# Row transposes on ScalarE's queue and half of the down products in 16 bits, in a decoder block with a mixture of experts

## The chip, the cores and the metric

The kernel runs on one core of a Trainium2 chip. The metric is the device time of one execution in microseconds (us). TensorE is PE in the profile (PEld is its weight load), VectorE DVE, ScalarE ACT, GpSimd POOL, SyncE SP.

## What is computed

One decoder block for 2048 tokens of width 1024, all float32. A first RMS norm, a projection, two token mixers (gated linear attention and causal pooling) merged by gates, and an output product added to x. Then a second RMS norm, whose rows feed a router (36 logits per token, one group of experts, the two best experts in it) and 32 experts of inner width 256:

```python
h2 = rmsnorm(x, norm2_g[l])
...
g_logits = (ht @ w_rg).astype(jnp.float32) + b_rg.astype(jnp.float32)
e_all = jnp.einsum('td,gde->tge', ht, w_re).astype(jnp.float32) + b_re.astype(jnp.float32)
...
return (jax.nn.silu(xb @ w_gate[e]) * (xb @ w_up[e])) @ w_down[e]
```

The expert rows are weighted, added to x by token, and normed once more.

## The kernel before

**Numbers in two halves.** A float32 operand is mostly kept as two float16 tiles, the rounded value (high half) and the rest (low half); a product is then three matmuls, high by high, high by low and low by high (`PASSES`). `msplit` (lines 1293 to 1298) does this to a tile of expert weights, 128 x 1024: ACT writes the high half (line 1296), DVE the low half (line 1297). Gate and up weights go that way (tiles `mst`, then `mwh`); the down weights (tiles `msd`) do not, and their products run in float32.

**Mixer, four blocks of 512 tokens.** `block` (line 887) runs for each. At its end `out_mm` computes the output product, 128 tokens (a tile, t0 to t3) at a time; `out_norm` stores the tile (`out_dram`), norms it (`normed`: sum of squares at line 240 on ACT, scaling at line 242 on DVE, high half at line 251 on ACT, low half at line 251 on DVE) and stores the halves (`h2d`) from POOL's queue. `out_turn` (line 869) calls `turn`, which transposes the two halves by DMA (line 259), two DMAs for each tile, on the queue named by `TQ`, that is SP's. SP's queue also carries all weight loads of the mixer (line 168), in the order in which they stand. `logits` (line 874) multiplies the transposed halves with the router's weights (line 881, tile `aux`). The logits of a block and its routing are done inside the next block, as fillers (`fill`) between the matmuls of its first projection (`seven_raw`, line 638). In the fourth block the order is another (`LAST`).

**Experts.** 32 experts in 16 pairs (`moe`, line 1220). The order within a pair is `PLAN`: S0 to S5 load and split the next pair's weights (`split1`), U and A are the gate and up products of one expert (`mo_up`, line 1391) and the activation (`mo_act`: sigmoid on ACT at line 1399, two products on DVE at lines 1400 and 1401), X are the transposes of the next pair's rows (lines 1335 and 1348), D0 and D1 the down product of 128 rows of either expert (`mo_out`, lines 1416 and 1419), D2 that of up to 56 more rows of each (`mo_rest`, lines 1428 and 1431: two products of 64 output rows side by side), F the last norm and the scatter. A scheduler in the compiler orders what is ready on each engine by its own estimates; the engines then keep that order. Pools hold 8 tiles `mst`, 8 tiles `mwh` and 8 tiles `msd`.

Of the kernel before, what the change touches and what calls it, by code (L numbers as in the profile page):

```python
# [8 lines left out]
F16 = mybir.dt.float16  # L9
BF16 = mybir.dt.bfloat16  # L10
I32 = mybir.dt.int32
AF = mybir.ActivationFunctionType
OP = mybir.AluOpType
# [3 lines left out]
D = 1024  # L17
# [5 lines left out]
CAP = 128 + RW  # L23
PW = 1024
EPS = 1e-6
WSC = 64.0
ASC = 16.0
DSC = 1.0 / (WSC * ASC)
RSC = 4096.0
# [7 lines left out]
class Mixer:  # L37
# [213 lines left out]
        self.done = [self.nc.scalar.activation(hh[0], x, AF.Copy).ins, eng.tensor_tensor(hh[1], x, hh[0], op=OP.subtract).ins]  # L251
        return hh

    def turn(self, hh, dst, dma):

        nc = self.nc
        if dma:
            for i in range(2):
                self.turning = getattr(nc, self.TQ).dma_start(dst(i), hh[i], transpose=True).ins
            return  # L260
        for i in range(2):
            pt = self.pp.tile([128, 1024], F16, name="acch", tag="acc", bufs=4)
            for k in range(KT):
                nc.tensor.transpose(pt[:, k * 128:(k + 1) * 128], hh[i][:, k * 128:(k + 1) * 128], self.identh)
            p3 = pt.rearrange("p (k t) -> p k t", k=KT)
            if i == 0:
                nc.scalar.activation(dst(i), p3, AF.Copy)
            else:
                nc.vector.tensor_copy(dst(i), p3)
# [598 lines left out]

    def out_turn(self, hh, dma):
        h2 = [self.bt([128, KT, 128], F16) for _ in range(2)]  # L870
        self.turn(hh, lambda i: h2[i], dma)
        return h2

    def logits(self, t, h2):
# [12 lines left out]
    def block(self, b, tail):  # L887
# [55 lines left out]
        if last:  # L943
# [15 lines left out]
            def fetch(i):  # L959
                with self.tc.issue_after(self.turning):  # L960
                    self.fetch(n, i)

            acts = {"m": lambda t: (mm(t, 0), mm(t, 1)) if t else mm(t, 1), "t": turn, "l": logits,
                    "n": lambda t: (mm(t, 0), mm(t, 1, lambda: turn(t - 1))),
                    "s": split, "f": fetch}
            for c in self.LAST.split():
# [11 lines left out]
        def wo1():  # L978
            wo[1] = [self.weight("wv", O0 + 4 + j) for j in range(4)]

        acts = {"m": lambda t: mm(t, 0), "n": lambda t: mm(t, 1), "t": turn, "w": lambda t: wo1(), "a": lambda t: self.p1a(), "b": lambda t: self.p1b(),
                "c": lambda t: self.p1c()}
        for c in self.OUT.split():
# [213 lines left out]
    def columns(self, T, nm, pool):  # L1197

        V = self.nc.vector
        p, n = T.shape[0], T.shape[2]  # L1200
        wsc = 1.0 / RSC if T.shape[1] > 2 else 1.0
        t = pool.tile([p, 2, n], F32, name="tj" + nm)
        ii = pool.tile([p, 2, n], I32, name="ti" + nm)
        w = pool.tile([p, n], F32, name="tw" + nm)
        l = pool.tile([p, 2, n], F32, name="tl" + nm)
        z = T[:, 0]
        V.scalar_tensor_tensor(t[:, 1], z, -1.0, z, op0=OP.mult, op1=OP.max)
        V.tensor_scalar(ii[:, 0], t[:, 1], 1.0, -1.0, op0=OP.max, op1=OP.add)
        V.tensor_scalar(t[:, 0], t[:, 1], 1.0, -1.0, op0=OP.max, op1=OP.add)
        V.tensor_scalar(t[:, 1], z, 0.0, OOB, op0=OP.is_equal, op1=OP.mult)  # L1210
        V.tensor_tensor(t[:, 1], t[:, 0], t[:, 1], op=OP.add)
        V.tensor_copy(ii[:, 1], t[:, 1])
        V.tensor_scalar(w, T[:, 1], wsc, None, op0=OP.mult)
        if T.shape[1] > 2:
            V.scalar_tensor_tensor(w, T[:, 2], wsc, w, op0=OP.mult, op1=OP.add)
        V.tensor_scalar(l[:, 0], z, 0.0, None, op0=OP.is_lt)
        return ii, w, l, t


    def moe(self):  # L1220
# [18 lines left out]
        with tc.manual_schedule(engines={getattr(E, e) for e in self.MANUAL}) if self.MANUAL else ExitStack():  # L1239
            for P in range(self.NP + 1):  # L1240
# [5 lines left out]
                for c in plan.split():  # L1246
                    f, d = {"U": (self.mo_up, 0), "V": (lambda s, h: self.mo_up(s, h, 0, 128), 0),
                            "W": (lambda s, h: self.mo_up(s, h, 128, CAP), 0), "A": (self.mo_act, 0), "D": (self.mo_down, 0), "F": (self.finish, 0),
                            "G": (self.finish, -1), "R": (self.rows, 2), "B": (self.base, 1), "X": (self.mo_x, 1),
# [19 lines left out]
    def weights(self, P):  # L1269

        return {"P": P, "e": [8 * (j % 4) + j // 4 for j in (2 * P, 2 * P + 1)], "W": {}, "F": {}, "X": {}, "H": {}, "ac": {}, "ps": {}}

# [9 lines left out]
    def split1(self, s, i):  # L1282
        if i in s["W"]:
            return
        if i not in s["F"]:
            self.fetch(s, i)
        s["W"][i] = s["F"][i] if i % 3 == 2 else [self.msplit(f, self.mw) for f in s["F"][i]]

    def split(self, s):
        for i in self.ORDER:  # L1290
# [1 line left out]

    def msplit(self, f, pool):
        nc = self.nc
        w = pool.tile([128, 2, PW], F16, name="mwh", bufs=8192 // PW)
        nc.scalar.activation(w[:, 0], f, AF.Copy, scale=WSC)  # L1296
        nc.vector.scalar_tensor_tensor(w[:, 1], f, WSC, w[:, 0], op0=OP.mult, op1=OP.subtract)  # L1297
        return w
# [4 lines left out]
        q = slice(c % PW, c % PW + n)  # L1303
        return w[c // PW][:, q] if a is None else w[c // PW][:, a, q]

    BST, BSD = 8192 // PW, 8192 // PW

    def rows(self, s, i):
        P = s["P"]
# [71 lines left out]
    def mo_up(self, s, h, lo=0, hi=CAP):  # L1381
        nc, mp = self.nc, self.mp
        W, xT = [s["W"][3 * h + i] for i in range(2)], s["xT"][:, h]
        pg, pu = s["pp"][h] if lo else (self.acc(), self.acc())
        s.setdefault("pp", {})[h] = pg, pu
        for o, ps in ((0, pg), (1, pu)):
            for c in range(2):
                for k in range(KT):
                    for i, (a, b) in enumerate(self.PASSES):
                        col = k * 256 + c * 128  # L1390
                        nc.tensor.matmul(ps[:, c * CAP + lo:c * CAP + hi], self.part(W[o], col, 128, a), xT[:, b, k, lo:hi],  # L1391
                                         start=k == 0 and i == 0, stop=k == KT - 1 and i == 2)
        s["ps"][h] = pg[:, :2 * CAP], pu[:, :2 * CAP]

    def mo_act(self, s, h):
        nc, mp = self.nc, self.mp
        pg, pu = s["ps"][h]
        sg = mp.tile([128, 2 * CAP], F32, name="sg", bufs=4)
        nc.scalar.activation(sg, pg, AF.Sigmoid, scale=DSC)
        nc.vector.scalar_tensor_tensor(sg, pg, DSC, sg, op0=OP.mult, op1=OP.mult)  # L1400
        nc.vector.scalar_tensor_tensor(sg, pu, DSC, sg, op0=OP.mult, op1=OP.mult)  # L1401
        s["ac"][h] = sg.rearrange("p (c t) -> p c t", c=2)

    def mo_down(self, s, i):
        x, o, w, l, nl = s["X"][i]
# [5 lines left out]
    def mo_out(self, s, i, x, w):  # L1411
        nc = self.nc
        for hf in range(2):
            ps = self.acc()
            for f in range(2):
                nc.tensor.matmul(ps, s["ac"][i][:, f, :128], self.part(s["W"][3 * i + 2], f * D + hf * 512, 512),  # L1416
                                 start=f == 0, stop=f == 1)
            xh = x[:, hf * 512:(hf + 1) * 512]
            nc.vector.scalar_tensor_tensor(xh, ps, w, xh, op0=OP.mult, op1=OP.add)  # L1419

    def mo_rest(self, s, x, w):

        nc = self.nc
        ps = self.acc()
        m = [(h, f) for h in range(2) for f in range(2)]
        for q, (h, f) in enumerate(m):
            for hf in range(2):
                nc.tensor.matmul(ps[hf * 64:(hf + 1) * 64], s["ac"][h][:, f, CAP - 64:],
                                 self.part(s["W"][3 * h + 2], f * D + hf * 512, 512),
                                 start=q == 0, stop=q == len(m) - 1, tile_position=(0, hf * 64))  # L1430
        nc.vector.scalar_tensor_tensor(x, ps, w, x, op0=OP.mult, op1=OP.add)

    def finish(self, s, i):
# [59 lines left out]
    def overflow(self):  # L1493

        nc, tc = self.nc, self.tc
        V = nc.vector
        mp = self.mp
        nt = self.NTT
        n = nc.values_load(self.tot[0:1, 0:1], min_val=0, max_val=2 * nt + NE,  # L1499
                           skip_runtime_bounds_check_because="counts of the rows bound it")  # L1500
        with tc.If(n > 0):
            with tc.For_i(0, n):
                T = lambda name, sh, dt=F32: mp.tile([128] + sh, dt, name="o" + name)
# [24 lines left out]
                for c in range(2 * nt):  # L1528
                    a = mp.tile([128, 128], F32, name="oA", bufs=1)
# [4 lines left out]
                ii, w, _, _ = self.columns(tb, "o", mp)  # L1534
                er = nc.values_load(ei[0:1, 0:1], engines=[mybir.EngineType.SP], min_val=0, max_val=NE - 1,
                                    skip_runtime_bounds_check_because="a count of at most 31")
                W = [[self.load(self.A["we"][bass.ds(er, 1), :, c:c + PW].rearrange("o p c -> p (o c)"), i == 2)
                      for c in range(i * 2048, (i + 1) * 2048, PW)] for i in range(3)]
                W = [[self.msplit(f, self.mw) for f in w] if i < 2 else w for i, w in enumerate(W)]
                x = self.mxs[0]  # L1540
                o = self.out, ii
                self.base1(x, o, True)
                h = self.mhs[0]
# [8 lines left out]
                s = {"W": W, "xT": xT, "ac": {}, "ps": {}}  # L1552
# [5 lines left out]
            n = nc.values_load(self.tot[0:1, 1:2], min_val=0, max_val=nt, skip_runtime_bounds_check_because="0 or all tiles")  # L1558
            with tc.For_i(0, n) as t:
                x = self.mxs[0]  # L1560
# [98 lines left out]
```

## Time and profile before

| | |
|---|---|
| time, median of 3 runs | 1652.97 us (1650.61 to 1653.81) |
| profiled execution | 1646.32 us, span 1644.5 us |
| PE busy | 1516.8 us (92% of the span) |
| PEld busy | 916.5 us (56%) |
| DVE busy | 1063.8 us (65%) |
| ACT busy | 648.3 us (39%) |
| POOL busy | 523.8 us (32%) |
| mean granted TensorE clock | 0.965 |

The four blocks of the mixer fill the first 1100 us or so, the router's tables and the start of the experts the next 90 us, the 16 pairs the stretch from about 1160 to 1628 us. "Busy" of PE is the union of its matmuls, which overlap, so that a full row does not by itself mean full speed; the granted clock stands beside it, 1.00 being 2.4 GHz and 0.50 1.2 GHz.

### The profile page before, as it was taken

The page shows a single profiled execution, that of the slowest core. Times are in us where ns is not written, and L with a number is a line of the kernel's source. Part 1 is how long each engine was busy: PE and PEld are TensorE (multiplying, and loading weights), DVE is VectorE, ACT ScalarE, POOL GpSimd, SP SyncE. Part 2 cuts the span into 40 slices and gives each one's busy share as a digit, 9 for nine tenths or more (in the row PEclk, how much of TensorE's full clock was granted, in tenths as well). Part 3 has the DMA queues.
Part 4 walks back from the last instruction along what each step waited for, and adds up shares of the span by engine and source line. Part 5 has one row for each costly group of instructions (what it writes and reads, how often), then busy time and mean ns, then how long its engine had stood idle before and what let it go on. Part 6 is the DMA issues. An engine that isn't in the chain of part 4 may idle for free. (4 is left out here: it accounts for less than half of the span.)

```text
span 1644.5 us, 27592 instructions
## 1 busy us (share of the span) xinstructions
PE 1516.8 (92%) x10635; PEld 916.5 (56%) x10635; DVE 1063.8 (65%) x1941; ACT 648.3 (39%) x1021; POOL 523.8 (32%) x499
## 2 busy tenths in 40 slices
PE   4889996998999999999998999996799999999995
PEld 2365442445844444854443764443678686877773
DVE  8999797356844446762624773337667777777772
ACT  5643454251122252122333121123456566666651
POOL 1044243312414311332412341031434434444431
PEclk9899999998999999999999999997899999999998
DMA  8866687999566969566879665668699999999940
GB/s 292 256 218 214 212 266 221 262 344 263 163 193 195 258 177 324 155 214 178 234 173 275 224 186 164 202 185 288 240 314 329 334 331 336 335 330 324 331 180 34
DMA packets 247336, 400.95 MB, mean 244 GB/s; under 512 B 154731, under 2 KB 159211, under 8 KB 247200
## 3 DMA queue, kind: packets, MB, share of 16 engines
q1 hardware_dynamic: 224672, 330.79, 65.0%
q0 software_dynamic: 22528, 68.35, 11.4%
q8 instruction: 85, 1.39, 0.3%
q14 instruction: 51, 0.42, 0.1%
HBM read 300.33 MB, written 75.50 MB: 229 GB/s over the span
## 5 line engine op out<-in xcount | busy, mean ns | idle before, releaser
L1391 PE MATMUL acc<-xT,mwh 128*128 128x184 f16 (+2 forms) x3264 | 248.9, 238 | 0.0
L1391 PEld LDWEIGHTS <-mwh 128*128 128x128 f16 x3264 | 243.7, 98 | 7.7 <-issue 7.5
L842 PE MATMUL acc<-w,bt 128*128 128x512 f16 x768 | 169.4, 382 | 9.2 <-ACT w L175 9.2
L859 PE MATMUL acc<-w,bt 128*128 128x512 f16 x768 | 168.8, 379 | 3.5 <-DMA bt<-bt 1.9
L1297 DVE SCALAR_TENSOR_TENSOR mwh<-mst,mwh 128x1024 f16<-128x1024 f32 x128 | 153.4, 1219 | 24.2 <-ACT mwh L1296 24.0
L1296 ACT ACTIVATE mwh<-mst 128x1024 f16<-128x1024 f32 x128 | 128.7, 1050 | 54.3 <-PE acc L1391 53.5
L522 PEld LDWEIGHTS <-w 128*128 128x128 f16 x1344 | 131.0, 99 | 33.7 <-issue 9.3
L842 PEld LDWEIGHTS <-bt 128*128 128x128 f16 x768 | 75.7, 99 | 102.3 <-issue 13.5
L339 PEld LDWEIGHTS <-hS 128*128 128x128 f16 x768 | 75.5, 98 | 95.3 <-issue 5.8
L859 PEld LDWEIGHTS <-bt 128*128 128x128 f16 x768 | 74.4, 98 | 95.6 <-issue 5.8
L176 DVE SCALAR_TENSOR_TENSOR w<-w 128x1024 f16<-128x1024 f32 x74 | 99.9, 1365 | 38.4 <-ACT w L175 38.4
L175 ACT ACTIVATE w<-w 128x1024 f16<-128x1024 f32 x74 | 75.3, 1030 | 116.1 <-DMA w<-in_wv_dram 39.3
L1416 PE MATMUL acc<-msd,sg 128*128 128x512 f32 x256 | 115.9, 605 | 0.3 <-DVE sg L1401 0.3
L847 POOL TENSOR_TENSOR et<-et 128x512 f32<-128x512 f32 x32 | 45.2, 1418 | 200.8 <-DVE et L845 167.0
L522 PE MATMUL acc<-hS,w 128*128 128x256 f16 x768 | 95.1, 277 | 4.5 <-DVE w L176 3.0
L339 PEld LDWEIGHTS <-hT 128*128 128x128 f16 x576 | 56.4, 98 | 71.3 <-issue 5.1
L769 ACT ACTIVATE bt<-et 128x512 f16<-128x512 f32 x48 | 30.0, 628 | 166.6 <-POOL et L847 104.2
L845 DVE SCALAR_TENSOR_TENSOR et<-acc,et 128x512 f32<-128x512 f32 x64 | 43.4, 689 | 76.5 <-PE acc L842 76.5
L339 PE MATMUL aux<-w,hS 128*128 128x512 f16 x384 | 89.7, 384 | 3.1 <-DVE et L757 2.5
L339 PE MATMUL acc<-w,hS 128*128 128x512 f16 x384 | 88.3, 379 | 0.0
L819 ACT ACTIVATE et<-et 128x512 f32<-128x512 f32 x64 | 39.6, 629 | 105.4 <-DVE et L348 105.3
L1416 PEld LDWEIGHTS acc<-msd,sg 128*128 128x128 f32 x256 | 47.8, 193 | 56.4 <-issue 46.8
(307 smaller groups left out, 2608.5 us busy)
## 6 DMA issues: line engine op xcount, KB each, us to landing
w<-wkeep SPq DMA_DIRECT2D x210, 512.0 KB, 4.5
mst<-in_we_dram SPq DMA_DIRECT2D x128, 512.0 KB, 6.2
wkeep<-w SPq DMA_DIRECT2D x70, 512.0 KB, 3.0
msd<-in_we_dram SPq DMA_DIRECT2D x64, 512.0 KB, 7.2
w<-in_wv_dram SPq DMA_DIRECT2D x40, 512.0 KB, 5.3
x<-in_x_dram SPq DMA_DIRECT2D x32, 512.0 KB, 5.9
out_dram<-x POOLq DMA_DIRECT2D x16, 512.0 KB, 8.2
h2d<-bt POOLq DMA_DIRECT2D x32, 256.0 KB, 6.2
```

The lines of the kernel that those rows point to most:

```text
L175: nc.scalar.activation(w[:, 0, c:], f[:, c:], AF.Copy, scale=WSC)
L176: nc.vector.scalar_tensor_tensor(w[:, 1, c:], f[:, c:], WSC, w[:, 0, c:], op0=OP.mult, op1=OP.subtract)
L339: nc.tensor.matmul(p, L[name](i, c, k), w[k // 2][:, a, (k % 2) * 512:(k % 2 + 1) * 512], start=k == 0 and m == 0, stop=k == 3 and m == 2)
L522: nc.tensor.matmul(ps[:, :h], w[:, i, k * 128:(k + 1) * 128], L[name](c, k), start=k == 0 and m == 0, stop=k == 3 and m == 2)
L842: nc.tensor.matmul(ps, lhs, w[k // 2][:, a, (k % 2) * 512:(k % 2 + 1) * 512], start=k == 0 and i == 0, stop=k == 3 and i == 2)
L845: nc.vector.scalar_tensor_tensor(x, ps, DSC * ASC, x, op0=OP.mult, op1=OP.mult)
L847: self.on('madd').tensor_tensor(x, x, s[t, 1], op=OP.add)
L859: nc.tensor.matmul(ps, self.mT[t][k // 4][:, 4 * c + k % 4], w[hf][k // 2][:, a, (k % 2) * 512:(k % 2 + 1) * 512], start=k == 0 and i == 0 ...
L1296: nc.scalar.activation(w[:, 0], f, AF.Copy, scale=WSC)
L1297: nc.vector.scalar_tensor_tensor(w[:, 1], f, WSC, w[:, 0], op0=OP.mult, op1=OP.subtract)
L1391: nc.tensor.matmul(ps[:, c * CAP + lo:c * CAP + hi], self.part(W[o], col, 128, a), xT[:, b, k, lo:hi], start=k == 0 and i == 0, stop=k == ...
L1416: nc.tensor.matmul(ps, s["ac"][i][:, f, :128], self.part(s["W"][3 * i + 2], f * D + hf * 512, 512), start=f == 0, stop=f == 1)
```

## The change

Two things are changed.

1. In the first three blocks `out_turn` gives the two transposes of each tile to ScalarE's queue; in the fourth they stay on SP's.
2. Of each pair, the first expert's down product (h = 0) runs on float16 halves, in three passes. Its down weights are split by `msplit` into a pool of 4 tiles, its activations are split into a tile `ac` (high half on ACT, low half on POOL). The second expert's stay float32. The pool of `msd` shrinks from 8 tiles to 6. The scale of the split weights (`WSC`) and activations (`ASC`) is taken back in the rows' weights (`DSC`) and, for the second expert, by leaving out a factor.

```diff
@@ turn, out_turn
-    def turn(self, hh, dst, dma):
+    def turn(self, hh, dst, dma, queue=None):
...
-                self.turning = getattr(nc, self.TQ).dma_start(dst(i), hh[i], transpose=True).ins
+                self.turning = getattr(nc, queue or self.TQ).dma_start(dst(i), hh[i], transpose=True).ins
...
-        self.turn(hh, lambda i: h2[i], dma)
+        self.turn(hh, lambda i: h2[i], dma, None if self.blk + 1 == self.NB else "scalar")
@@ columns
-        wsc = 1.0 / RSC if T.shape[1] > 2 else 1.0
+        wsc = DSC / RSC if T.shape[1] > 2 else DSC
@@ split1, msplit
-        s["W"][i] = s["F"][i] if i % 3 == 2 else [self.msplit(f, self.mw) for f in s["F"][i]]
+        s["W"][i] = s["F"][i] if i == 5 else [self.msplit(f, self.mq if i == 2 else self.mw) for f in s["F"][i]]
...
-        w = pool.tile([128, 2, PW], F16, name="mwh", bufs=8192 // PW)
+        w = pool.tile([128, 2, PW], F16, name="mwh", bufs=(8192 if pool is self.mw else 4096) // PW)
...
-    BST, BSD = 8192 // PW, 8192 // PW
+    BST, BSD = 8192 // PW, 6144 // PW
@@ mo_act
-        nc.vector.scalar_tensor_tensor(sg, pu, DSC, sg, op0=OP.mult, op1=OP.mult)
-        s["ac"][h] = sg.rearrange("p (c t) -> p c t", c=2)
+
+        nc.vector.scalar_tensor_tensor(sg, pu, 1.0 if h else DSC * ASC, sg, op0=OP.mult, op1=OP.mult)
+        sg = sg.rearrange("p (c t) -> p c t", c=2)
+        s["ac"][h] = sg
+        if h == 0:
+            ac = s["ac"][h] = mp.tile([128, 2, 2, CAP], F16, name="ac", bufs=2)
+            nc.scalar.activation(ac[:, 0], sg, AF.Copy)
+            nc.gpsimd.tensor_tensor(ac[:, 1], sg, ac[:, 0], op=OP.subtract)
+
+    def downs(self, s, h):
+
+        ac, w = s["ac"][h], s["W"][3 * h + 2]
+        for f in range(2):
+            for a, b in self.PASSES if h == 0 else ((None, None),):
+                yield ac[:, f] if h else ac[:, b, f], lambda hf: self.part(w, f * D + hf * 512, 512, a)
@@ mo_out, mo_rest
-            for f in range(2):
-                nc.tensor.matmul(ps, s["ac"][i][:, f, :128], self.part(s["W"][3 * i + 2], f * D + hf * 512, 512),
-                                 start=f == 0, stop=f == 1)
+            n = 5 if i == 0 else 1
+            for q, (a, w2) in enumerate(self.downs(s, i)):
+                nc.tensor.matmul(ps, a[:, :128], w2(hf), start=q == 0, stop=q == n)
...
-        m = [(h, f) for h in range(2) for f in range(2)]
-        for q, (h, f) in enumerate(m):
+        for q, (a, w2) in enumerate(x for h in range(2) for x in self.downs(s, h)):
             for hf in range(2):
-                nc.tensor.matmul(ps[hf * 64:(hf + 1) * 64], s["ac"][h][:, f, CAP - 64:],
-                                 self.part(s["W"][3 * h + 2], f * D + hf * 512, 512),
-                                 start=q == 0, stop=q == len(m) - 1, tile_position=(0, hf * 64))
+                nc.tensor.matmul(ps[hf * 64:(hf + 1) * 64], a[:, CAP - 64:], w2(hf),
+                                 start=q == 0, stop=q == 7, tile_position=(0, hf * 64))
```

(The overflow loop, which runs no iteration with these inputs' row counts unless an expert has too many rows, splits its down weights as well.)

What the change moves, at three places. First ACT, where the first block hands over to the second: line 240 is the sum of squares of t2 and then t3, line 251 the high half of t2 and then t3, line 259 the transposes of t0 (the first two), t1, t2 and t3.

```order
+L259 DMA_TRANSPOSE bt_2835<-bt_2761 128x8x128
+L259 DMA_TRANSPOSE bt_2836<-bt_2762 128x8x128
 L240 ACTIVATE bt_2866,nss_2867<-x_2600 128x1024
 L251 ACTIVATE bt_2873<-x_2600 128x1024
+L259 DMA_TRANSPOSE bt_2879<-bt_2829 128x8x128
+L259 DMA_TRANSPOSE bt_2880<-bt_2830 128x8x128
 L240 ACTIVATE bt_2910,nss_2911<-x_2655 128x1024
 L251 ACTIVATE bt_2917<-x_2655 128x1024
+L259 DMA_TRANSPOSE bt_2923<-bt_2873 128x8x128
+L259 DMA_TRANSPOSE bt_2924<-bt_2874 128x8x128
+L259 DMA_TRANSPOSE bt_2927<-bt_2917 128x8x128
+L259 DMA_TRANSPOSE bt_2928<-bt_2918 128x8x128
```

The eight transposes now stand between ACT's steps of the later tiles' norms. Second SP's queue at the same place; line 168 is a weight load, line 273 the load of a tile of x for the next block.

```order
 L168 DMA w_3426<-wkeep_79 128x2048
-L259 DMA_TRANSPOSE bt_2835<-bt_2761 128x8x128
-L259 DMA_TRANSPOSE bt_2836<-bt_2762 128x8x128
 L168 DMA w_3428<-wkeep_79 128x2x512
+L273 DMA x_4644<-in_x_dram 128x1024
 L168 DMA w_3534<-wkeep_79 128x2048
-L273 DMA x_4644<-in_x_dram 128x1024
-L259 DMA_TRANSPOSE bt_2879<-bt_2829 128x8x128
-L259 DMA_TRANSPOSE bt_2880<-bt_2830 128x8x128
 L273 DMA x_4787<-in_x_dram 128x1024
-L259 DMA_TRANSPOSE bt_2923<-bt_2873 128x8x128
-L259 DMA_TRANSPOSE bt_2924<-bt_2874 128x8x128
```

The transposes leave SP's queue (two more go behind the last row), and the loads behind them close up. Third DVE in the experts, from the end of one pair's D2 (line 1431) to the first gate tiles of a later pair. Before:

```order
L1431 SCALAR_TENSOR_TENSOR mx2_10495<-acc_13652,twr_10526,mx2_10495 128x512
L1460 TENSOR_TENSOR frs_13641<-frs_13641,tlm_10509 128x1
L1486 COPY frs_13663<-fss_13662 64x1
L1487 COPY frs_13663<-fss_13662 64x1
L1488 TENSOR_TENSOR fss_13662<-fss_13662,frs_13663 128x1
L1489 TENSOR_SCALAR frs_13663<-fss_13662 128x1
L1467 TENSOR_TENSOR y_13642<-mx1_10494,y_13642 128x1024
L1460 TENSOR_TENSOR frs_13663<-frs_13663,tlr_10527 128x1
L1297 SCALAR_TENSOR_TENSOR mwh_13682<-mst_13678,mwh_13682 128x1024
```

Now, at the same place of the changed kernel (its line 1443 is the old 1431, its 1298 the old 1297):

```order
L1443 SCALAR_TENSOR_TENSOR mx2_10495<-acc_13825,twr_10526,mx2_10495 128x512
L1298 SCALAR_TENSOR_TENSOR mwh_13883<-msd_13879,mwh_13883 128x1024
L1298 SCALAR_TENSOR_TENSOR mwh_13886<-msd_13881,mwh_13886 128x1024
L1479 TENSOR_TENSOR y_13815<-mx1_10494,y_13815 128x1024
L1498 COPY frs_13844<-fss_13843 64x1
L1499 COPY frs_13844<-fss_13843 64x1
L1298 SCALAR_TENSOR_TENSOR mwh_13863<-mst_13859,mwh_13863 128x1024
```

The two new splits of down weights stand between D2 and the pair's last norm, ahead of the next gate tiles.

## Rows read from the trace of the kernel before

**Rows 1.** Windows: start:end, us, busy (count) by engine, PEclk, DMA share, GB/s.

```profile
1250.00:1300.00 50.00, 50.00 (x504) 39.46 (x503) 37.58 (x63) 32.88 (x45) 19.28 (x21) 1.00 0.94 333
```

**Rows 2.** Timeline of PE, one pair: start us, us, engine, line, operation, tiles, count.

```profile
1313.73 15.12 PE L1391 MATMUL acc<-xT,mwh 128*128 128x184 f16 x189
...
1330.09 7.08 PE L1416 MATMUL acc<-msd,sg 128*128 128x512 f32 x16
...
1337.99 3.65 PE L1428 MATMUL acc<-msd,sg 128*64 128x512 f32 x16
...
1342.04 1.19 PE L1391 MATMUL acc<-xT,mwh 128*128 128x184 f16 x13
```

**Rows 3.** Waits of PE: waited for, us in total, times, longest us.

```profile
PE aux L881 <- DMA bt<-bt: 18.3, 7, 4.7
```

**Rows 4.** Timeline of PE, after the first, second and third block.

```profile
365.62 2.75 PE L638 MATMUL acc<-w,hS 128*128 128x512 f16 x12
...
380.62 0.21 PE L881 MATMUL aux<-wrh,bt 128*128 128x36 f16 x1 [4.72 <-DMA bt<-bt]
...
380.70 5.22 PE L638 MATMUL aux<-w,hS 128*128 128x512 f16 x12
...
634.36 4.44 PE L638 MATMUL aux<-w,hS 128*128 128x512 f16 x12
...
897.42 4.57 PE L638 MATMUL aux<-w,hS 128*128 128x512 f16 x12
```

**Rows 5.** Windows around those three bursts.

```profile
380.60:386.00 5.40, 5.38 (x24) 2.10 (x25) 0.04 (x1) 0.00 (x0) 0.00 (x0) 0.52 1.14 255
634.30:638.70 4.40, 4.40 (x22) 1.73 (x19) 0.20 (x1) 0.83 (x1) 0.00 (x0) 0.61 1.08 369
893.00:901.00 8.00, 4.47 (x33) 2.11 (x34) 2.62 (x6) 1.28 (x1) 0.00 (x0) 0.58 1.17 377
```

**Rows 6.** Timeline of SP's queue, after the first block.

```profile
359.30 10.01 SPq L259 DMA_TRANSPOSE bt<-bt  x2
...
371.48 7.86 SPq L259 DMA_TRANSPOSE bt<-bt  x2
...
380.07 6.11 SPq L259 DMA_TRANSPOSE bt<-bt  x4
```

**Rows 7.** Transposes on SP's queue by line: ns of issue min/median/max, first and last start.

```profile
L259 SPq DMA_TRANSPOSE bt<-bt x28: 1232/2188/8660, 359.3 to 1114.9; - x28
```
```profile
L771 SPq DMA_TRANSPOSE bt<-bt x48: 1232/1245/2527, 138.3 to 1088.4; - x48
```

**Rows 8.** DMA, 340 to 366 us: traffic; issues, KB each, median us to landing.

```profile
DMA packets 2958, 10.69 MB, mean 411 GB/s; under 512 B 353, under 2 KB 353, under 8 KB 2956
...
w<-wkeep SPq DMA_DIRECT2D x8, 512.0 KB, 15.7
out_dram<-x POOLq DMA_DIRECT2D x4, 512.0 KB, 10.2
...
bt<-bt SPq DMA_TRANSPOSE x1, 11.7
```

**Rows 9.** Timeline of ACT, after the first block: high halves of t0 and t1.

```profile
358.80 1.05 ACT L251 ACTIVATE bt<-x 128x1024 f16<-128x1024 f32 x1
...
364.31 1.06 ACT L251 ACTIVATE bt<-x 128x1024 f16<-128x1024 f32 x1 [3.42 <-DVE x L242]
```

**Rows 10.** Costliest groups: count, busy us, mean ns, idle us before, its releaser.

```profile
L842 PE MATMUL acc<-w,bt 128*128 128x512 f16 x768 | 169.4, 382 | 9.2 <-ACT w L175 9.2
L1297 DVE SCALAR_TENSOR_TENSOR mwh<-mst,mwh 128x1024 f16<-128x1024 f32 x128 | 153.4, 1219 | 24.2 <-ACT mwh L1296 24.0
L1296 ACT ACTIVATE mwh<-mst 128x1024 f16<-128x1024 f32 x128 | 128.7, 1050 | 54.3 <-PE acc L1391 53.5
L847 POOL TENSOR_TENSOR et<-et 128x512 f32<-128x512 f32 x32 | 45.2, 1418 | 200.8 <-DVE et L845 167.0
```

More of the change, by code (lines that the diff above doesn't have):

```diff
@@ L1538, in overflow @@
                       for c in range(i * 2048, (i + 1) * 2048, PW)] for i in range(3)]
-                W = [[self.msplit(f, self.mw) for f in w] if i < 2 else w for i, w in enumerate(W)]
+                W = [[self.msplit(f, self.mw if i < 2 else self.mq) for f in w] for i, w in enumerate(W)]
                 x = self.mxs[0]
```

## The prediction

> **What bounds the kernel now.** I began with the experts, because both halves of the change meet TensorE and most of its float32 work is there. The window of 50 us inside the pairs [rows 1] is to be read from left to right: PE is busy for 50.00 of 50.00 us at a granted clock of 1.00, that is at 2.4 GHz, while DVE has 37.58, ACT 32.88 and POOL 19.28. DMA is busy for 0.94 of it at 333 GB/s. So here a microsecond taken from PE is a microsecond of the kernel, as long as no other engine comes last. The timeline of one pair [rows 2] gives the period, 1342.04 - 1313.73 = 28.31 us, and what the down products have in it: D0 and D1 together 7.08 us, D2 3.65 us, all in float32. Per period DVE works 37.58 / 50 x 28.31 = 21.28 us, ACT 18.62, POOL 10.92.
>
> For the mixer I read the waits of PE. The largest wait on a DMA there is that of the router's logits for the transposed rows, 18.3 us in 7 waits [rows 3]. The timeline of PE at the three handovers between blocks [rows 4] shows a second price: a burst of twelve matmuls takes 2.75 us before the waits and 5.22, 4.44 and 4.57 us behind them, and the windows around these bursts grant a clock of 0.52, 0.61 and 0.58 [rows 5], so TensorE runs mostly at 1.2 GHz after having waited. That is 2.47 + 1.69 + 1.82 = 6.0 us more. Together 24.3 us hang on these transposes, and no more than that can be won from them.
>
> Why they are late is seen on SP's queue [rows 6]: the pair of t0 holds it for 10.01 us, that of t1 for 7.86, the last four for 6.11, 24 us in all. The same operation issued in quieter stretches (line 771) has a median of 1.245 us, and line 259's here 2.188 with 8.66 at most [rows 7]. Just before, the DMAs moved 411 GB/s, eight weight loads stood ahead on the same queue, landing 15.7 us after issue, and the first transpose took 11.7 us to land, while POOL's queue landed transfers of the loads' size in 10.2 [rows 8].
>
> **Part 2, the first expert's down product in 16 bits.** Half of D0 and D1 goes: 3.54 us. In its place stand 12 float16 matmuls of 128 x 512 (2 halves of the width, 2 chunks of the inner width, 3 passes). The same shape in the mixer costs 169.4 / 768 = 0.2206 us each [rows 10], so 2.65 us: -0.89. Half of D2 goes: 1.83 us. In its place stand 12 matmuls with 64 output rows. If two run side by side, as the float32 ones do in being 3.65 us where eight full ones would be 7.08, each costs 0.110: 1.32 us, -0.50. If they do not, they cost 2.65, +0.82. No row shows float16 matmuls of this shape; I take side by side, the nearest row being the same shape in float32, and keep the other end. The period falls by 1.39 to 26.92 us, and by 16 pairs 22.3 us. At the other end it is 0.07 x 16 = 1 us.
>
> What is added lies beside PE. Each pair has two more splits, 2 x 1.05 = 2.10 us on ACT and 2 x 1.22 = 2.44 on DVE, and the activations' own split: on ACT 1.05 x 368 / 1024 = 0.38 us, on POOL 1.42 x 368 / 512 = 1.02 [rows 10]. (368 columns are two times 184, the width of the gate and up products in [rows 2].) DVE comes to 23.72 of 26.92 us (88%), ACT to 21.10 (78%), POOL to 11.94 (44%). The same bytes in a shorter period need 333 x 28.31 / 26.92 = 350 GB/s, below the 411 that were reached [rows 8]. The activations' split is hidden by the second expert's gate and up products, half of the 15.12 us of both [rows 2], against 0.38 + 1.02 and the passing on. The splits of down weights stand on DVE between D2 and the next gate tiles; behind them wait the next pair's gate splits, by 2.44 us, and the last norm of the pair. I price this at nothing as long as DVE's 3.2 us of rest per pair absorbs it; that is the point of a rival below. The two `msd` tiles fewer cost nothing, because the tiles of the first expert are now free once they are split and no longer held until D2. The first pair has no period to save in, and the three-pass chains are longer; for these I take off 2.3 us: **-20**.
>
> **Part 1, the transposes on ACT.** 24 DMAs go from SP's queue to ACT's, and with them their issue time. Between which bounds: 1.25 us each as on the quiet stretches, or what they cost on SP here, up to 24 us per handover. The nearest row is that of line 259 itself, whose median is 2.19 us; ACT's queue carries no weight loads ahead of them, so I take 1.25 to 2.19.
>
> ACT has room, but not for nothing. t0's pair follows the high half of t1, which ends at 359.85 [rows 9], about when SP issues it today. Then ACT's square sum of t2 waits, by 2.5 to 4.4 us, and with it the chain to t2's high half (now 364.31 [rows 9]), behind which t1's pair stands. t1's pair is then issued between 368 and 374 and lands, with the 3 to 4 us that ACT's own steps and the transfer still want, at 374 to 377, where the logits get it now at 380.62 [rows 4]. **What is late next** is t2 and t3: their high halves move back by 5 to 9 us, so that their pairs are issued at about 376 to 383, where SP began at 380.07 [rows 6]. So t0's and t1's waits go nearly whole, and part of it comes back as a wait for t2. The loads behind them on SP close up; nothing on PE waits for these there. Bounds: 0, and -24.3. I take a bit over half: **-13**.
>
> **Sum.** -20 - 13 = -33 us. The profiled execution, 1646.3 us, becomes 1613.3; it lies 6.7 us below the median of the runs, 1653.0, on which the forecast is made: 1620.
>
> **Rivals.**
> - *The queue was not the cause.* If the transposes land late because all 16 DMA engines are full (411 GB/s [rows 8]) and not because of what stands ahead on SP's queue, part 1 is worth 0: 1633. For it speaks the 11.7 us landing with the DMAs full; against it the shorter landings of POOL's queue at the same time. The Trainium skill speaks for this rival ("DMA: Bandwidth & Descriptors", section "Issuing engines are not separate DMA queues"): DMAs of all issuing engines run on the same 16 DMA engines, and issuing from several saves only the sequencer's time. By that rule the 24 us of issue per handover could go and the landing could not; the trace agrees as to the full engines and, by POOL's 10.2 against 15.7, not as to the landing. Chance 0.16.
> - *Half of part 2 is lost* because DVE at 88% delivers the splits late now and then: -10 in place of -20: 1630. For it: DVE's split already waits 24.0 us for ACT's half [rows 10]. Chance 0.13.
> - *16-bit matmuls of 64 rows do not run side by side*: part 2 is -1: 1639. Chance 0.03.
> - *Slower: ACT is held by its own transposes.* If they cost on ACT what they cost on SP [rows 6], t0's pair ends at 370, and t2's square sum, t2's high half, t1's pair and so on follow in a chain: t3's pair would end at about 397, against 386 today. That is up to 8 us later in the logits per handover, +24 with -20: 1657. It decides from an issue time of some 3 us each. For it: ACT issues in order, and the chain of the norm runs through it. Against it: nothing stands ahead of them on that queue. Chance 0.05.
> - *Slower: DVE becomes the bound of the pair.* Its rest is now 28.31 - 21.28 = 7.03 us; if this rest is waiting in order that cannot be shortened, the period is 23.72 + 7.03 = 30.75, +2.44 x 16 = +39, with -13: 1679. It decides when over 5.4 of the 7.03 us must remain (26.92 - 23.72 = 3.2 are there for nothing, and 2.2 more use up both gains). Against it: PE's 50.00 of 50 shows that DVE waits for PE, not PE for DVE. Chance 0.04.
>
> **How the numbers follow.** The forecast has 0.59; its own range runs from all of part 1 and part 2 (1653 - 24.3 - 22.3 = 1606) to a third of part 1 (1629). The range 1606 to 1638 takes in the first two rivals and leaves out 0.12 of the others and a little of each end. About 0.2% (3.3 us) is what a measurement can tell from no change. Faster: 0.59 + 0.16 + 0.13 + 0.03, less 0.01 for bad mixtures: 0.90. Slower: 0.04 and most of 0.05: 0.07; the same, 0.03.
>
> **What the profile afterwards would show.** Right: DMA transposes of line 259 on ACT's queue at 1.25 to 2.2 us; the logits' wait for `bt` down from 18.3 to some 5 to 10 us; bursts of 2.75 us behind them for part of the handovers; a pair period of 26.9 us with PE still at 50 of 50; float16 down matmuls at 0.22 us and, in D2, at 0.11; DVE at some 88%. Wrong: issue times of 4 us and more on ACT, ACT steps of t2 and t3 later by 8 us or more; PE below 49 of 50 in a pair with waits on DVE or on the tile `ac`; a D2 of 4.5 us.

## The result and the profile after

The changed kernel takes 1676.53 us (median of 4 runs, 1672.07 to 1685.67) against 1653.12 before: ratio 1.0153, 95% interval 1.0128 to 1.0178. It is **slower by some 23 us**, where 1620 (1606 to 1638) was forecast. The profiled execution is longer than that of before by 32.3 us (spans 1676.8 and 1644.5), and the places below are for that pair of executions.

Where the time went is found by looking for the same matmul in both traces. The middle one of line 339's matmuls of the second, third and fourth block starts 10.2, 28.8 and 42.0 us later than before: each handover between blocks loses 10 to 19 us. The end of D2 of the first pair is 46.8 us later, of the last pair 32.0. So the mixer lost 42 us, the start of the experts 5, and the pairs won 15.

**The experts first.** The window in the pairs, as [rows 1], and the timeline of PE over one pair, as [rows 2]:

```profile
1350.00:1400.00 50.00, 50.00 (x546) 40.93 (x545) 44.32 (x70) 40.26 (x53) 26.44 (x24) 1.00 0.99 354
```
```profile
1325.84 1.88 PE L1441 MATMUL acc<-msd,sg 128*64 128x512 f32 x8
...
1345.05 2.76 PE L1431 MATMUL acc<-mwh,ac 128*128 128x512 f16 x12
1347.65 3.60 PE L1431 MATMUL acc<-msd,sg 128*128 128x512 f32 x8
...
1351.87 1.49 PE L1441 MATMUL acc<-mwh,ac 128*64 128x512 f16 x12
1353.19 1.88 PE L1441 MATMUL acc<-msd,sg 128*64 128x512 f32 x8
```

PE is still full, DVE at 89%, DMA at 354 GB/s. The twelve 16-bit matmuls take 2.76 us, those of 64 rows 1.49: they do run side by side. From D2 to D2 it is 1353.19 - 1325.84 = 27.35 us. But it does not stay there: six pairs on, the same piece of D2 starts at 1490.02 and then at 1518.53, 28.51 us apart, and PE falls below 50 of 50:

```profile
1450.00:1500.00 50.00, 49.05 (x485) 36.96 (x483) 42.53 (x67) 34.19 (x48) 27.05 (x24) 1.00 0.96 347
```

**The mixer.** The logits' wait, [rows 3], has not shrunk but doubled; the view by source line shows the transposes on ACT's queue, as [rows 7] on SP's:

```profile
PE aux L882 <- DMA bt<-bt: 38.4, 11, 8.8
```
```profile
L259 ACTq DMA_TRANSPOSE bt<-bt x24: 1248/1472/15171, 357.7 to 936.1; - x24
```

Half of them take under 1.5 us to issue, as hoped; the longest 15.17. What a long one does is seen in ACT's timeline after the first block, to be read beside [rows 9]:

```profile
357.67 1.36 ACTq L259 DMA_TRANSPOSE bt<-bt  x1
...
359.02 1.05 ACT L251 ACTIVATE bt<-x 128x1024 f16<-128x1024 f32 x1
360.77 7.85 ACTq L259 DMA_TRANSPOSE bt<-bt  x1
368.67 1.06 ACT L240 ACTIVATE bt<-x 128x1024 f16<-128x1024 f32 x1 [8.60 <-issue]
...
372.05 1.06 ACT L251 ACTIVATE bt<-x 128x1024 f16<-128x1024 f32 x1 [2.23 <-DVE x L242]
...
378.29 13.76 ACTq L259 DMA_TRANSPOSE bt<-bt  x4
```

The second transpose of t0 holds ACT for 7.85 us; the square sum of t2 waits 8.60 us for it, t2's high half comes at 372.05 (before: 364.31; the two steps in [rows 9] are the high halves of t1 and t2, not of t0 and t1), and the last four are issued until 392.05 (before: 386.18 [rows 6]).

The waits are not all of the loss. The windows from the last matmul of line 859 to the middle one of line 339 in the next block, at the second handover, before and after (columns as in [rows 1]):

```profile
608.57:763.43 154.86, 150.79 (x1011) 90.73 (x1009) 92.58 (x214) 32.12 (x82) 46.81 (x46) 0.99 0.71 218
```
```profile
618.77:792.22 173.45, 155.52 (x1011) 92.56 (x1009) 92.88 (x214) 32.22 (x82) 46.10 (x46) 0.94 0.70 194
```

As many matmuls (1011) keep PE busy for 4.7 us longer, at a granted clock of 0.94 in place of 0.99, and the other 13.9 us are idle. Over the three handovers PE is idle for 27 us more and busy for 15 us more.

Why is the transpose slow with nothing ahead of it? The DMA view of 362 to 366 us, while it is being issued, and of 390.5 to 392.5, by queue (packets, MB, share of 16 engines); q10 is ACT's, q1 SP's, q0 POOL's:

```profile
q1 hardware_dynamic: 352, 1.27, 77.4%
q0 software_dynamic: 80, 0.26, 16.1%
q10 hardware_dynamic: 354, 0.09, 10.0%
```
```profile
q10 hardware_dynamic: 2189, 0.54, 126.5%
```

Alone, ACT's queue moves 2189 packets in 2 us. Beside SP's loads it moves 354 in 4 us while SP moves 352: as many as SP, as if they went one by one in turn. Most of SP's are 4 KB (159 ns each), a transpose is 1024 packets of 256 bytes (18 ns). At 88 a microsecond one transpose would last some 12 us. **Theory A** is that queues with work take turns at the DMA engines, packet by packet. The Trainium skill has it as a rule ("DMA: Bandwidth & Descriptors", section "Queues, rings and completion order"): each DMA engine goes round between the queues that have work, a packet at a time. The counts, 354 to 352, agree. By theory A the loads behind a transpose on SP's own queue do not come between its packets, and POOL's stores still can.

And SP, which no longer issues these transposes, waits for them. Of its waits from 600 to 670 us these two did not stand there before:

```profile
SPq L273 <- DMA bt<-bt: 17.3, 1, 17.3
SPq L168 <- DMA bt<-bt: 12.4, 1, 12.4
```

Rivals: **B**, ACT's queue is itself slow at transposes; **C**, what counts is that ACT is held and the norms stand behind it, whoever shares the engines; **D**, what counts is that SP's loads and ACT's transposes now wait for each other.

### The profile page after: what moved, and what is told of

It reads as the page before. It is cut to its first block, busy times and chain, and to the rows that moved or that the text cites. A ratio compares the mean times of both kernels' runs of the same rounds, so it can differ in the third digit from the quotient of the medians.

```text
span 1676.8 us, 28015 instructions
## 1 busy us (share of the span) xinstructions
PE 1517.0 (90%) x10763; PEld 920.6 (55%) x10763; DVE 1102.2 (66%) x1973; ACT 682.5 (41%) x1069; POOL 564.0 (34%) x515
## 5 line engine op out<-in xcount | busy, mean ns | idle before, releaser
L1298 DVE SCALAR_TENSOR_TENSOR mwh<-mst,mwh 128x1024 f16<-128x1024 f32 x128 | 159.5, 1275 | 8.5 <-ACT mwh L1297 8.2
L842 PEld LDWEIGHTS <-bt 128*128 128x128 f16 x768 | 75.6, 98 | 100.4 <-issue 11.1
L522 PE MATMUL acc<-hS,w 128*128 128x256 f16 x768 | 100.4, 286 | 7.3 <-ACT w L175 2.3
L210 POOL TENSOR_TENSOR rms<-rms,mhalf 128x1 f32<-128x1 f32 (+1 forms) x44 | 39.7, 903 | 140.6 <-DVE rms L209 139.7
L770 POOL TENSOR_TENSOR bt<-et,bt 128x512 f16<-128x512 f32 x48 | 61.7, 1288 | 43.0 <-ACT bt L769 43.0
```

Of the source, the lines that this page charges most:

```text
L522: nc.tensor.matmul(ps[:, :h], w[:, i, k * 128:(k + 1) * 128], L[name](c, k), start=k == 0 and m == 0, stop=k == 3 and m == 2)
L770: self.on(lo).tensor_tensor(hl[:, 1], x, hl[:, 0], op=OP.subtract)
L842: nc.tensor.matmul(ps, lhs, w[k // 2][:, a, (k % 2) * 512:(k % 2 + 1) * 512], start=k == 0 and i == 0, stop=k == 3 and i == 2)
```

## Experiments

Ratios are to runs of the kernel before on the same chip, whose medians lay between 1647.6 and 1653.1 us.

**Each part alone.** `act_alone` is the kernel before with the edits of `turn` and `out_turn`; `down16_alone` the changed kernel with

```diff
-        self.turn(hh, lambda i: h2[i], dma, None if self.blk + 1 == self.NB else "scalar")
+        self.turn(hh, lambda i: h2[i], dma, None)
```

> The kernel before with the first part alone: the 24 transposes on ACT's queue. In the changed kernel the mixer ends 42 us later than before (10, 18.6 and 13.4 us at the three handovers) and the pairs win about 15. If the whole loss is made by the transposes (theory A: on a queue of their own their 1024 packets of 256 bytes each alternate with the 4 KB packets of SP's loads, and behind them stands ACT's norm chain), this kernel takes 1653 + 42 = 1695 us. Rival: part of the loss in the mixer comes from the second part (other tiles, other order); then under 1680.

> The changed kernel with the transposes back on SP's queue: the second part alone. From the changed profile: 16 pairs 15 us shorter, the start of the first pair 5 us longer: 1653 - 15 + 5 = 1643 us. If the mixer's delay was what made the first pair late, 1638. As forecast at first (-20): 1633. If the pairs lose their gain without part one: 1653.

Part one: 1694.7 us, ratio 1.0285 (1.0256 to 1.0314), some 46 us lost. Part two: 1636.51, ratio 0.9925 (0.9898 to 0.9952), 12.6 us won. So the whole loss is part one's. (The parts add up to +33, the change to +23; part one's runs spread from 1689 to 1711, and what is left was not followed.)

**Whose fault is the queue?** `loads_pool` leaves the transposes on SP and issues the loads of line 168 from POOL's queue:

```diff
-        nc.sync.dma_start(w[:, :, c:], self.C[self.kept[mat, i]][:, :, c:])
+        nc.gpsimd.dma_start(w[:, :, c:], self.C[self.kept[mat, i]][:, :, c:])
```

> The kernel before with the mixer's weight loads of line 168 issued from POOL's queue; the transposes stay on SP's. Theory A (two queues share the DMA engines packet by packet): now SP's transposes run beside loads of another queue and get slow as ACT's were, the longest issues 8 to 15 us, the pairs over 8 us wherever 4 KB packets flow, though nothing stands ahead of them on SP. Rival B (ACT's queue itself is slow at transposes): SP's take 1.25 to 2.2 us, since the loads that stood ahead are gone. The total is not forecast: POOL's norm steps stand behind its loads.

1729.13 us, in a single run whose total was not forecast; what counts is its trace. The view by source line, and the DMA view of 368 to 378 us, by queue:

```profile
L259 SPq DMA_TRANSPOSE bt<-bt x28: 1232/4802/12267, 361.8 to 1192.3; - x28
```
```profile
q0 software_dynamic: 1051, 3.70, 93.1%
q1 hardware_dynamic: 1052, 0.28, 12.5%
```

SP's transposes became slow (median 4.80 us, longest 12.27) although no weight load stood ahead of them: 1051 packets on POOL's queue, nearly all of loads, and 1052 on SP's, nearly all of transposes. B falls.

**Is holding ACT needed for the loss?** `late_two_act` gives ACT only t2's and t3's transposes, behind which no norm stands:

```diff
...
-        self.turn(hh, lambda i: h2[i], dma)
+        self.turn(hh, lambda i: h2[i], dma, "scalar" if t > 1 and self.blk + 1 < self.NB else None)
```

> The kernel before, with only the transposes of the last two tiles (t2, t3) of the first three blocks on ACT's queue: behind them stands no step of the norms. If the loss is mostly ACT held in front of its norm steps (theory C), at most 3 us per handover are left: 1650 to 1662. If it is the packets' sharing alone (theory A without C), the four take some 13 us where SP's took 6 to 10, 4 to 7 us per handover: 1665 to 1675. In both, issue times of 4 to 10 us where loads flow.

1675.32 us, ratio 1.0151 (1.0117 to 1.0185): at the upper end of theory A's range (just past it), 13 us outside C's. The logits' wait:

```profile
PE aux L881 <- DMA bt<-bt: 42.3, 11, 8.7
```

Two times from the timelines, in us after the block's last matmul of line 859, at the three handovers, tell holding and sharing apart:

| | end of t3's high half (ACT) | end of the last logits (PE) |
|---|---|---|
| before | 28.1, 18.8, 22.7 | 52.6, 39.2, 43.2 |
| the change | 36.6, 29.9, 27.4 | 60.5, 55.9, 53.8 |
| `late_two_act` | 28.1, 17.7, 22.7 | 55.4, 53.9, 53.3 |
| `act_gated` | 23.7, 18.4, 20.4 | (loads late) |
| `sp_stores` | 29.1, 14.8, 14.0 | 48.0, 36.8, 37.6 |

With the norms on time as before, 27.6 of the change's 35.2 us are still lost. So most of the loss does not need ACT to be held. What holding adds is not separated, because `late_two_act` also leaves half of the transposes on SP.

**Take the competitor away.** `act_gated` is part one alone; each load of line 168 that is written behind a tile's transposes waits until they have landed:

```diff
-        nc.sync.dma_start(w[:, :, c:], self.C[self.kept[mat, i]][:, :, c:])
+        ins = nc.sync.dma_start(w[:, :, c:], self.C[self.kept[mat, i]][:, :, c:]).ins
+        if self.gate is not None:
+            self.tc.add_manual_dep(ins, self.gate.name, mybir.DependencyInfo(
+                mybir.DependencyClass.Sync, mybir.DependencyReason.DATA), reason="gate")
...
+        self.gate = self.turning if self.blk + 1 < self.NB else None
```

> Part one alone, with every weight load of line 168 that is written behind a tile's transposes (of the first three blocks, up to the next block's second stage) made to wait until these have landed, as on SP's queue it would stand behind them. Theory A (three queues take turns packet by packet; without SP's loads only POOL's stores are left): the slow issues on ACT fall from 8 to 16 us to the 3 to 8 us of SP's queue and at least half of the 42 us goes: 1655 to 1673. Rival C (what counts is that ACT is held and that the norms stand behind it, whoever shares the engines): 1685 to 1700. If the loads are missed by PE more than the rows, more than 1700.

1746.3 us, ratio 1.0548 (1.0513 to 1.0582), the last case named. The view by source line, ACT's timeline after the first block (line 262 is the old 259, 243 the old 240), and PE's largest wait:

```profile
L262 ACTq DMA_TRANSPOSE bt<-bt x24: 1247/1680/8694, 353.2 to 969.4; - x24
```
```profile
354.71 1.27 ACTq L262 DMA_TRANSPOSE bt<-bt  x1
356.03 1.06 ACT L243 ACTIVATE bt<-x 128x1024 f16<-128x1024 f32 x1 [1.37 <-issue]
```
```profile
PE aux L641 <- DMA w<-wkeep: 125.3, 3, 45.2
```

On the point it was made for it is clear: t0's second transpose, 7.85, 15.17 and 12.22 us at the three handovers of the change, takes 1.27, 1.35 and 1.36; t2's square sum waits 1.37 us in place of 8.60; t3's high half is earlier than before (table). Without SP's weight loads ACT's queue is quick there. It is not quick throughout: the longest issue is 8.69 us, behind t3's high half, where POOL's stores and rows of x still flow. The total says nothing on that, because PE now waits 125 us for loads: too many were held back.

**Smaller packets.** `act_2kb` issues each load of line 168 as two (halves of 2 KB a packet), on top of part one; `sp_2kb` does the same to the kernel before.

```diff
-        nc.sync.dma_start(w[:, :, c:], self.C[self.kept[mat, i]][:, :, c:])
+        for k in range(2):
+            nc.sync.dma_start(w[:, k, c:], self.C[self.kept[mat, i]][:, k, c:])
```

> Part one alone again (24 transposes on ACT's queue), but each weight load of line 168 is issued as two, one for each half, so that its packets are 2 KB in place of 4 KB; the bytes are the same. Theory A (the transposes' packets alternate one by one with the other queue's packets): a transposed packet now waits for half as long, the slow issues fall from 8 to 16 us to some 5 to 8, and about half of the 42 us of loss goes: 1665 to 1680. If it is bytes that are shared, or ACT's queue that is slow, or only its being held: 1690 to 1700 as with 4 KB.

> The control for it: the kernel before, transposes on SP's queue, the same loads in two halves of 2 KB packets. The loads of SP's own queue still stand ahead and nothing alternates with them but POOL's stores: 1649, within 6 us either way. If 2 KB packets are slower for the loads, more, and that is then to be taken off the other run.

1695.92 (ratio 1.0298, 1.0272 to 1.0324) and 1654.09 (1.0036, 1.0016 to 1.0055). **A miss**: the longest issue is still 13.4 us and no time came back. The stores of POOL and the loads of x kept their 4 KB packets. In that issue (632.5 to 645.9 us) ACT's queue moves 910 packets and SP's 1000, again nearly one to one, and POOL's 441 take 38.9% of the engines' time; whether smaller stores would help was not tried. The size of the loads' packets alone is no lever here.

**Other ways to turn the rows.** `pe_turns` is `down16_alone` with the transposes of the first three blocks on PE; `sp_stores` is `down16_alone` with POOL's stores of these blocks on SP's queue, so that no other queue is left at the handovers:

```diff
-        self.nc.gpsimd.dma_start(self.out[rows, :], self.xo[t])
+        (self.nc.gpsimd if self.blk + 1 == self.NB else self.nc.sync).dma_start(self.out[rows, :], self.xo[t])
...
-                nc.gpsimd.dma_start(store[:, i, :], hh[i])
+                (nc.gpsimd if self.blk + 1 == self.NB else nc.sync).dma_start(store[:, i, :], hh[i])
```

> The second part of the change, and in the first three blocks the row transposes on PE (16 matmuls of 128 x 128 for each tile and copies by ACT and DVE) and not by DMA at all: 12 tiles x 16 x 0.06 = 11.5 us more on PE, 24 us of waits and half clock less: 1636 - 12 = 1624. Rival: the copies stand in ACT's and DVE's norm chain and PE waits for them in place of the DMA: 1636 or more.

> The second part alone, with the stores of the first three blocks (rows of x and their normed halves) on SP's queue in place of POOL's: at the handovers SP's is then the only queue, and no transposed packet alternates with another queue's. Theory A: transposes that have come to their turn take 1.25 us each, the largest issue is below 4 us but for the loads ahead; the total may fall below 1637 by up to 10 us, unless SP, held by stores that wait for the norm, brings the loads late: then 1640 to 1660.

`pe_turns`: 1665.76, ratio 1.0104 (1.0085 to 1.0124), the rival: PE now waits for ACT's high halves, 22.3 us in 7 waits, in place of the DMA. `sp_stores`: **1618.02 us, ratio 0.9799 (0.9782 to 0.9815), faster than both kernels.** Its transposes and the logits' wait:

```profile
L259 SPq DMA_TRANSPOSE bt<-bt x28: 1232/1707/4095, 361.4 to 1100.8; - x28
```
```profile
PE aux L882 <- DMA bt<-bt: 12.4, 8, 6.2
```

The longest issue is 4.10 us (8.66 in [rows 7]), the logits end 2.4 to 5.6 us earlier at each handover, as theory A would have it. But the run moves a second thing. DVE's scaling of a tile (line 242) waits for the tile's store to land; the kernel before, then `sp_stores`:

```profile
DVE x L242 <- DMA out_dram<-x: 25.8, 7, 7.0
```
```profile
DVE x L242 <- DMA out_dram<-x: 13.4, 5, 7.1
```

With the stores on SP's queue this wait falls to about half, and t3's high half is 4.0 and 8.7 us earlier at the second and third handover (table). What shorter issues and what earlier stores won was not separated. Two runs on it:

> The changed kernel (transposes on ACT's queue, 16 bits) with the stores of the first three blocks on SP's queue: against the run with the stores and the transposes on SP (1618) only the queue of the transposes differs. Theory A: SP's loads and stores still take turns with ACT's packets and ACT is still held in front of its norm steps: slow issues of 5 to 12 us remain, 1640 to 1662. Rival: POOL's stores alone made ACT's transposes slow: 1616 to 1625, no slow issues.

> The kernel before with nothing changed but the stores of the first three blocks, on SP's queue. If the gain of the run with stores and 16 bits (1618 against 1637 with 16 bits alone) is the transposes' and independent of the experts: 1651 - 18 = 1633. If half of it came from the experts (its late pairs kept 27.2 us for longer): 1637 to 1642.

`act_sp_stores`: 1683.06, ratio 1.0206 (1.0161 to 1.0251); its longest issue is 7.61 us and yet it is slower than either side forecast. The length of the issues is thus not all that counts: summed over the 24 transposes of the handovers they take 82.8 us on SP's queue before, 95.6 in the change and 73.8 here, less than before. What the trace shows beside them is waiting between the queues (D): the first transpose of t2 has been issued on ACT at 654.1, its low half is done on DVE at 654.5, and the second is issued only at 664.09; SP's loads wait 15.8 us for transposes to land in that handover. Such waits of SP stand at every handover of the change (9.1, 29.7 and 20.1 us) and at none before or in `sp_stores`. How much of the loss is theirs, and what imposes them, was not tried: D stays open beside theory A. `stores_alone`: 1640.54, ratio 0.9930 (0.9913 to 0.9947), 10.8 us of the 18 expected and inside the range for half of the gain being the experts' (1637 to 1642). From the first D2 to the last the pairs take 403.1 us in `sp_stores` and 406.9 in `down16_alone`, so some 4 us are theirs. The 16 bits on top of `stores_alone` are worth 1640.5 - 1618.0, some 22 us.

**Why the late pairs stretch.** In `pool_mult` the product of the last norm goes from DVE to POOL for two of three row tiles, in `act_cast` a copy of the row transposes from DVE to ACT, in `stores_ac_dve` (on `sp_stores`) the activations' low half from POOL to DVE:

```diff
-        nc.vector.tensor_tensor(y, x, y, op=OP.mult)
+        (nc.gpsimd if i < 2 else nc.vector).tensor_tensor(y, x, y, op=OP.mult)
...
-                self.evac(a, xT[:, :, a, k0:k0 + 4, 128:].rearrange("p h k t -> p k h t"),
+                self.evac(0, xT[:, :, a, k0:k0 + 4, 128:].rearrange("p h k t -> p k h t"),
...
-            nc.gpsimd.tensor_tensor(ac[:, 1], sg, ac[:, 0], op=OP.subtract)
+            nc.vector.tensor_tensor(ac[:, 1], sg, ac[:, 0], op=OP.subtract)
```

> The second part alone, with the last product of the norm (128 x 1024, two of three row tiles of a pair) on POOL in place of DVE: 2.4 us less on DVE per pair, 5.6 more on POOL. If the late pairs (periods of 28.0 to 29.0 in place of 27.2) are late because DVE falls behind, they come back to 27.2: 1636 - 6 = 1630. Rival: something else stretches them (loads, PE itself): 1636; or POOL becomes late with the scatters: 1640 and more.

> The second part alone, with one copy of the row transposes per pair (128 x 448 from PSUM, 0.62 us) moved from DVE to ACT. If DVE's lag is what stretches the late pairs from 27.2 to 28 or 29 us, the lag of some 0.8 us per pair shrinks by 0.6 and 3 to 5 us are won: 1637 - 4 = 1633. If something else stretches them: 1637.

> Stores on SP's queue and 16 bits as in the best run, with the low half of the activations (128 x 368) made by DVE in place of POOL. If POOL's operation costs more by lengthening DVE's splits (1.22 to 1.30 us, 8 per pair) than DVE's own 0.55 us, the late pairs shorten: 1612 to 1617. If DVE's count is what matters, it gets later by 0.55 us per pair: 1620 to 1626.

`pool_mult` is a clear loss: 1660.9, ratio 1.0088 (1.0066 to 1.0109), against 0.9925 without it. `act_cast`: 1635.19, ratio 0.9888 (0.9871 to 0.9905), between its two forecasts; its late pairs still take up to 29 us, so the copy alone is not the cause. `stores_ac_dve`: 1622.56, ratio 0.9820 (0.9802 to 0.9839), not to be told from `sp_stores`. What they do show is in the groups of DVE's gate and up splits from 1300 to 1500 us: first the change; then `pool_mult`, with its splits of down weights and one of its one-column steps below; then `stores_ac_dve`:

```profile
L1298 DVE SCALAR_TENSOR_TENSOR mwh<-mst,mwh 128x1024 f16<-128x1024 f32 x56 | 70.2, 1286 | 0.9 <-ACT mwh L1297 0.8
```
```profile
L1298 DVE SCALAR_TENSOR_TENSOR mwh<-mst,mwh 128x1024 f16<-128x1024 f32 x54 | 69.7, 1319 | 2.4 <-ACT mwh L1297 2.1
L1298 DVE SCALAR_TENSOR_TENSOR mwh<-msd,mwh 128x1024 f16<-128x1024 f32 x14 | 23.7, 1704 | 1.7 <-ACT mwh L1297 1.5
...
L1472 DVE TENSOR_TENSOR frs<-frs,tlr 128x1 f32<-128x1 f32 x6 | 9.6, 1597 | 4.2 <-POOL frs L1502 4.2
```
```profile
L1298 DVE SCALAR_TENSOR_TENSOR mwh<-mst,mwh 128x1024 f16<-128x1024 f32 x56 | 66.6, 1218 | 0.4 <-ACT mwh L1297 0.4
```

A split of 1219 ns before [rows 10] takes 1286 ns where POOL has the activations' low halves, and 1218 again without them; one kind of one-column step on DVE (6 of them) goes from 256 ns in `down16_alone` to 1597 with POOL's long products. So POOL's elementwise work lengthens DVE's here. That it is what stretches the late pairs is not shown: with it gone the total stayed.

## Why the prediction was wrong

- **Part one, forecast -13, measured +46: the step that failed** is "ACT's queue carries no weight loads ahead of them, so I take 1.25 to 2.19". What stands ahead was half of the question. In the kernel before it did hold SP: during t0's first issue, 6.83 us from 359.3 on, 588 packets of loads and 14 of transposes went through SP's own queue. But what flows beside on another queue counts as well: t0's second transpose takes 7.85 to 15.17 us on ACT with SP's loads beside it and 1.27 to 1.36 without (`act_gated`), and SP's transposes get as slow beside POOL's loads (`loads_pool`). How the slow issues become the 46 us is open in part (D).
- The rule that I set against the forecast, that the engines are shared whoever issues, was taken to end at 0. It has a worse end: on ACT's queue a transpose moves no more packets than the loads beside it (354 to 352), where before, on SP's, 2450 packets of transposes went through from 383.5 to 386 with no load among them. The 8.66 us of [rows 7] already had this in their first half, beside POOL's stores (879.7 to 884); in the second SP's own loads stood ahead.
- The rival "ACT is held by its own transposes" had the place and the chain right (t3's high half later by 8.5, 11.1 and 4.7 us), and a chance of 0.05. Its price, +24 at most, was taken from SP's issue times as an upper bound; single issues went past them (15.17 us against 8.66). And `late_two_act` shows 28 us lost at the logits with no norm held.
- "The loads behind them on SP close up; nothing on PE waits for these": SP's loads and rows of x wait for the transposes to land, 29.7 us in one handover.
- The clock: after waits twelve matmuls still take 5.29 us at 391.09 in PE's timeline (granted clock 0.50, that is 1.2 GHz), as in [rows 4]. No wait went, so none of the 6.0 us came back, and more was lost: PE is busy for 15 us more over the three handovers, at 0.94 to 0.95 in place of 0.96 to 0.99. The 24.3 us were a bound for what could be won; what could be lost had none.
- **Part two, forecast -20, measured -12.6**: the working stood. 1.39 us a pair were forecast; the steady period, from D2 to D2, is 27.1 to 27.35 against 28.5 to 28.7 before. The 28.31 of the prediction was a little short, the saving was not. The 16-bit matmuls cost about what was said (2.76 us for 2.65, in D2 1.49 for 1.32), two of 64 rows side by side. Missing are some 5 us at the start of the first pair, where 2.3 had been taken off, and some 6 in the late pairs. There DVE's rest was to absorb the splits, priced at nothing; DVE is busy for 84 to 89% of the time, and the gain held only for the first eight pairs. What stretches the late ones is open. On top of `stores_alone` the part is worth some 22 us.
- The slower rival on DVE did not come: PE is at 50 of 50 in the early pairs.

## What to carry to other kernels

Be wary of moving a transfer of many small packets to a queue of its own while another queue carries large ones: here they got as many packets through as the large ones did and no more, and the engine that issued them was held for up to 15.17 us. Before moving a DMA off a busy queue, count the packets per queue in the window where it runs: what competes beside it matters as well as what stands ahead. Then look whether the old queue comes to wait for the new one. Here the opposite move, the other queue's stores on the transposes' queue, won 11 us alone and 35 with the 16-bit products, in part perhaps by landing the stores earlier.

## What was not expected of the hardware

A DMA transpose of 128 x 1024 in 16 bits is 1024 packets of 256 bytes: over 1000 a microsecond alone, 88 beside SP's 4 KB packets (and a few of POOL's). Halving the packets of the weight loads did not help. One elementwise POOL instruction per pair (128 x 368) lengthened the mean of DVE's splits by 5%, longer ones (128 x 1024, 2.42 us) one kind of DVE's one-column steps sixfold.
